# A router softmax on one core: VectorE and ScalarE run register loops over one softmax group a trip, and SyncE passes one word per load

## The chip, the cores and the metric

The kernel runs on one core of one Trainium2 chip. The time is the device time of one execution in microseconds (us); lower is better. The time of a kernel is the median over several executions. One further execution is recorded by the hardware profiler; its span (first to last recorded instruction) is a little shorter than its device time.

## The reference

```python
def setup_inputs():
    batch, seq, dim = 16, 512, 1024
    num_loras = 8
    return {
        "x": np.random.randn(batch, seq, dim).astype(np.float32),
        "router_weights": np.random.randn(dim, num_loras).astype(np.float32),
    }

def reference(x, router_weights):
    logits = np.matmul(x, router_weights)
    exp_logits = np.exp(logits - np.max(logits, axis=-1, keepdims=True))
    return (exp_logits / np.sum(exp_logits, axis=-1, keepdims=True)).astype(np.float32)
```

8192 tokens of 1024 values are multiplied with a 1024x8 matrix, and a softmax over the 8 results of each token follows. `x` is 33.55 MB, the output 0.26 MB.

## The kernel before

**Tiling.** Each of the 128 partitions holds 64 tokens. "Row j" below is the j-th token of all 128 partitions, a 128x1024 tile; there are 64 rows (J = 64). The list LOADS cuts rows 0 to 62 into transfers: 13 of four rows, three of two, five of one. Row 63 comes in three pieces of 512, 256 and 256 columns (PIECES).

**Loads.** The first four rows are loaded as fp32 by SyncE's DMA queue (L131) and cast to bf16 by ScalarE (`cast`, L333). All others are loaded by GpSimd's queue (L169, L182), which converts to bf16 on the way. GpSimd issues them one behind the other and has issued the last at about 17 us; from then on the DMA engines work the list down by themselves. Each of the 16 DMA engines adds 1 to a load's semaphore when its part has landed; 16 means landed.

**TensorE.** For a row it makes eight 128x128 transposes (a "turn", L276): five into the PSUM tile `ptv`, three into `pts`. VectorE copies `ptv` to SBUF (`dve_copy`, L376), ScalarE copies `pts` (`act_copy`, L350). Then TensorE makes eight small matmuls ("multiply", L263) whose result is 128x8 logits. There are two of each buffer. TensorE runs this as a loop of two rows a trip (L287 to L297) with the addresses in registers: two filler matmuls that keep the clock up, multiply of an odd row, a branch, turn of the next odd row, multiply of an even row, a wait for `s_in`, turn of the next even row, and the branch back (L297).

**Gates.** SyncE tells TensorE when a row has landed, row by row (L150 to L157). For an even row it adds 1 to `s_in`, for which TensorE waits ahead of the turn. For an odd row it waits until the buffer before was transposed (`s_tv`) and adds 1 to `s_c[1]`; TensorE's odd multiply waits for 3 there: the two copies of its own row and SyncE's word for the next odd row.

**Softmax.** After every eight rows (the first group has four) VectorE takes the maximum (L386), subtracts it (L390), ScalarE takes the exponential (L341), and VectorE sums, inverts and scales (L397, L401, L405), one of these steps behind each of the next rows' copies. VectorE and ScalarE have their whole program written out, one instruction per step and row. The tiles of a group come in pairs, used in turn.

**The end.** Rows 60 to 63 are handled alone (L303 to L328 on TensorE, L412 and L418 on VectorE, L343 on ScalarE). Row 63's pieces are transposed as they land (L310), copied out (VectorE L420, ScalarE L365), and multiplied (L324). Then come maximum, exponential, sum, inverse and scale of the last rows (L414, L345, L445, L447, L449), and the last 48 KB go out (L162). The first 208 KB go out at L160 when row 63's first piece has landed.

Of the kernel before, what the change touches and what calls it, by code (L numbers as in the profile page):

```python
# [11 lines left out]
def kernel(  # L12
# [6 lines left out]
    nc = tc.nc  # L19
    P = 128  # L20
    B, S, D = x.shape
    D2, N = router_weights.shape
    assert D2 == D
    M = B * S
    KO = D // P
    J = M // P
# [5 lines left out]
    fp32 = mybir.dt.float32  # L32
    bf16 = mybir.dt.bfloat16
    Exp = mybir.ActivationFunctionType.Exp
    X = mybir.AxisListType.X
    ALU = mybir.AluOpType
# [3 lines left out]
    LOADS = [4] * 13 + [2, 2, 2] + [1] * 5  # L40
    PIECES = [4, 2, 2]
    G, SKIP = 8, 4
    TRIPS = 31
    LOOP_T = 2 * TRIPS
    ALONE = 4
    NG = (J - ALONE + SKIP) // G
    starts = [max(0, G * g - SKIP) for g in range(NG)]
    ends = [G * (g + 1) - SKIP for g in range(NG)]
    DONE = ends[-2]
    assert sum(LOADS) == J - 1 and sum(PIECES) == KO and ends[-1] == J - ALONE  # L50
    VN, SN = 5, 3

    place = [16640]

    def sb(name, shape, dtype):
        size = mybir.dt.size(dtype)
        for n in shape[1:]:
            size *= n
        at = place[0]
        place[0] = -(-(at + size) // 64) * 64  # L60
        return nc.alloc_sbuf_tensor_at(name, shape, dtype, offset=at).ap()
# [8 lines left out]
    ident = sb("ident", [P, P], fp32)  # L70
    w8 = sb("w8", [KO, P, N], fp32)
    w_bf = sb("w_bf", [P, KO, N], bf16)
    outv = sb("outv", [P, J, N], fp32)
    filler = sb("filler", [P, 512], bf16)
    xTv = [sb(f"xTv{i}", [P, VN, P], bf16) for i in range(2)]
    xTs = [sb(f"xTs{i}", [P, SN, P], bf16) for i in range(2)]
    xTz = [sb(f"xTz{i}", [P, n, P], bf16) for i, n in enumerate(PIECES)]
    mx = [sb(f"mx{i}", [P, G, 1], fp32) for i in range(2)]
    ex = [sb(f"ex{i}", [P, G, N], fp32) for i in range(2)]
    ev = [sb(f"ev{i}", [P, G, N], fp32) for i in range(2)]  # L80
    ssum = [sb(f"ssum{i}", [P, G, 1], fp32) for i in range(2)]
    inv = [sb(f"inv{i}", [P, G, 1], fp32) for i in range(2)]
    low = sb("low", [P, ALONE], fp32)
    ev3 = sb("ev3", [P, ALONE, N], fp32)
    sum3 = sb("sum3", [P, ALONE, 1], fp32)
# [3 lines left out]
    LG_AT = 0x2000000  # L89
    lg = ps("lg", [P, 2, G, 64], fp32)  # L90
# [5 lines left out]
    sem = tc.alloc_semaphore  # L96
# [4 lines left out]
    s_ld = [sem(f"s_ld{i}") for i in range(len(LOADS))]  # L101
    s_z = [sem(f"s_z{i}") for i in range(len(PIECES))]
    s_cast = sem("s_cast")
    s_m = sem("s_m")
    s_d = sem("s_d")
# [5 lines left out]
    s_tv = sem("s_tv")  # L111
    s_ts = sem("s_ts")
    s_c = [sem(f"s_c{i}") for i in range(2)]
    s_in = sem("s_in")
    s_zt = [sem(f"s_zt{i}") for i in range(len(PIECES))]
    s_zc = [sem(f"s_zc{i}") for i in range(len(PIECES))]
    s_p = sem("s_p")
    s_ex = sem("s_ex")
    s_ev = sem("s_ev")
    s_low = sem("s_low")  # L120
    s_e3 = sem("s_e3")
    s_out = sem("s_out")
    s_st = [sem(f"s_st{i}") for i in range(2)]

# [21 lines left out]

    sp = nc.sync


    for j in range(2, J - 1):  # L150
        if j % 2:
            sp.wait_ge(s_tv, j - 1)
        if j < LOADS[0]:
            sp.wait_ge(s_cast, j + 1)
        elif j in first:
            sp.wait_ge(s_ld[first.index(j)], 16)
        sp.sem_inc(s_c[1] if j % 2 else s_in, 1)  # L157
    sp.wait_ge(s_z[0], 16)
    sp.wait_ge(s_out, NG - 1)
    sp.dma_start(out=out_rows[:, 0:DONE, :], in_=outv[:, 0:DONE, :]).then_inc(s_st[0], 16)  # L160
# [26 lines left out]
    pe = nc.tensor  # L187
# [22 lines left out]

    def loop_turn(b):

        for c in range(KO):
            t = again(
                turn_like,
                ins=(turn_like.ins[0], at([[J * D, P], [1, P]], xa, r_x[c])),
                outs=(pe.lower_ap(turn_ap(b, c), opt=False),),
            )
            if c == VN - 1:
                t.then_inc(s_tv, 1)  # L220
            if c == KO - 1:
                t.then_inc(s_ts, 1)
        pe.reg_add(r_l, r_l, 256)
        for c in range(KO):
            if c == KO // 2:
                pe.reg_alu(r_l, r_l, -4097, ALU.bitwise_and)
            pe.reg_add(r_x[c], r_x[c], D * 2)
# [7 lines left out]
                t.then_inc(s_ts, 1)  # L235
        return t

    def multiply(b, dst, want=2):

        for c in range(KO):  # L240
            if c == 0:
                pe.wait_ge(s_c[b], want).then_inc(s_c[b], -want)
            if dst is None:
                m = again(
                    mult_like,
                    ins=(
                        pe.lower_ap(w_bf[:, c, :], opt=False),
                        pe.lower_ap(chunk(b, c), opt=False, for_matmul_weights=True),
                    ),
                    outs=(at([[2 * G * 64, P], [1, N]], lg, r_l),),  # L250
                    start_tensor_calc=(c == 0),
                    stop_tensor_calc=(c == KO - 1),
                )
            else:
                m = pe.matmul(  # L255
                    dst, lhsT=chunk(b, c), rhs=w_bf[:, c, :],
                    start=(c == 0), stop=(c == KO - 1),
                )
            if c == KO - 1:
                m.then_inc(s_p, 1)  # L260
# [2 lines left out]
        return pe.matmul(spare, lhsT=filler[:, 0:P], rhs=filler, start=True, stop=True)  # L263


    w_ps = lg[:, 1, 0:N, 0:KO]
    pe.wait_ge(s_id, 1)
    pe.wait_ge(s_w, 16).then_inc(s_w, -16)  # L268
    for n in range(N):
# [2 lines left out]
    pe.wait_ge(s_fill, 1)  # L272
    mult_like = fill().ins
    pe.wait_ge(s_idb, 1)
    pe.wait_ge(s_cast, 2)
    turn_like = pe.transpose(turn_ap(0, 0), xa[:, 0, 0:P], identity).ins  # L276
    turn(0)
    pe.wait_ge(s_wb, 1)
# [8 lines left out]
    with nc.body("rows_multiply", valid_engines=only_pe):  # L287
        fill()
        fill()
        multiply(1, None, want=3)  # L290
        pe.br("rows_turn")
    with nc.body("rows_turn", valid_engines=only_pe):
        loop_turn(1)
        multiply(0, None)
        pe.wait_ge(s_in, 1).then_inc(s_in, -1)
        loop_turn(0)
        pe.br_lt(r_x[0], left_of(TRIPS - 1), on_true="rows_multiply", on_false="rows_done")  # L297
    nc.switch_bb("rows_done")
# [34 lines left out]
    def cast(i):  # L333
        act.wait_ge(s_f[i], 16).then_inc(s_f[i], -16)  # L334
        for k in (2 * i, 2 * i + 1):
            act.copy(xa[:, k, :], x_f32[:, k, :]).then_inc(s_cast, 1)  # L336

    def power(g):
        n = ends[g] - starts[g]
        act.wait_ge(s_ex, g + 1)  # L340
        act.activation(ev[g % 2][:, 0:n, :], ex[g % 2][:, 0:n, :], func=Exp).then_inc(s_ev, 1)  # L341

    def power_alone(k):  # L343
        act.wait_ge(s_low, k + 1)
# [1 line left out]
            ev3[:, k, :], alone[k], func=Exp, bias=low[:, k:k + 1]  # L346
        ).then_inc(s_e3, 1)

    def act_copy(j):
        act.wait_ge(s_ts, j + 1)  # L350
        act.copy(xTs[j % 2], pts[j % 2][:, 0:SN, :]).then_inc(s_c[j % 2], 1)  # L351

    cast(0)
    for j in range(J - 3):
        act_copy(j)
        if j == 1:
            cast(1)
        if j - 1 in ends[:-1]:
            power(ends.index(j - 1))
    power(NG - 1)  # L360
    act_copy(J - 3)
    power_alone(0)
    act_copy(J - 2)
    act.wait_ge(s_zt[0], 1)
    act.copy(xTz[0], z_bank[0]).then_inc(s_zc[0], 1)  # L365
    for k in range(1, ALONE):
# [6 lines left out]
    dve.wait_ge(s_wt, 1)  # L373
    dve.tensor_copy(out=w_bf, in_=w_ps.rearrange("p n ko -> p ko n")).then_inc(s_wb, 1)

    def dve_copy(j):  # L376
        dve.wait_ge(s_tv, j + 1)
        dve.tensor_copy(out=xTv[j % 2], in_=ptv[j % 2][:, 0:VN, :]).then_inc(s_c[j % 2], 1)  # L378

    def group(g):  # L380
        b, n = g % 2, ends[g] - starts[g]
        rows = lg[:, b, G - n:G, 0:N]

        def peak():
            dve.wait_ge(s_p, ends[g])
            dve.reduce_max(mx[b][:, 0:n, 0], rows, axis=X).then_inc(s_d, 1)  # L386

        def diff():
            dve.wait_ge(s_d, 3 * g + 1)
            dve.tensor_tensor(  # L390
                out=ex[b][:, 0:n, :], in0=rows, in1=mx[b][:, 0:n, :].broadcast_to([P, n, N]),
                op=ALU.subtract,
            ).then_inc(s_ex, 1)

        def total():
            dve.wait_ge(s_ev, g + 1)
            dve.reduce_sum(ssum[b][:, 0:n, 0], ev[b][:, 0:n, :], axis=X).then_inc(s_d, 1)  # L397

        def recip():
            dve.wait_ge(s_d, 3 * g + 2)  # L400
            dve.reciprocal(inv[b][:, 0:n, :], ssum[b][:, 0:n, :]).then_inc(s_d, 1)  # L401

        def scale():
            dve.wait_ge(s_d, 3 * g + 3)
            dve.tensor_tensor(  # L405
                out=outv[:, starts[g]:ends[g], :], in0=ev[b][:, 0:n, :],
                in1=inv[b][:, 0:n, :].broadcast_to([P, n, N]), op=ALU.mult,
            ).then_inc(s_out, 1)

        return [peak, diff, total, recip, scale]  # L410

    def low_alone(k):  # L412
        dve.wait_ge(s_p, J - ALONE + k + 1)
        dve.reduce_max(  # L414
            low[:, k:k + 1], alone[k], axis=X, negate=True
        ).then_inc(s_low, 1)
# [2 lines left out]
        dve.wait_ge(s_zt[i], 1)  # L419
        dve.tensor_copy(out=xTz[i], in_=z_bank[i]).then_inc(s_zc[i], 1)  # L420

    later = []
    for j in range(J - 3):
        dve_copy(j)
        if j in ends[:-1]:
            later += group(ends.index(j))
        if later:
            later.pop(0)()
    assert not later
    peak, diff, total, recip, scale = group(NG - 1)  # L430
    peak()
    diff()
    dve_copy(J - 3)
    total()
    low_alone(0)
    recip()
    dve_copy(J - 2)
    low_alone(1)
    dve_piece(1)
    dve_piece(2)  # L440
# [2 lines left out]
    scale()  # L443
    dve.wait_ge(s_e3, ALONE)
    dve.reduce_sum(sum3[:, :, 0], ev3, axis=X).then_inc(s_d, 1)  # L445
    dve.wait_ge(s_d, 3 * (NG) + 1)
    dve.reciprocal(inv3, sum3).then_inc(s_d, 1)  # L447
    dve.wait_ge(s_d, 3 * (NG) + 2)
    dve.tensor_tensor(  # L449
        out=outv[:, J - ALONE:J, :], in0=ev3, in1=inv3.broadcast_to([P, ALONE, N]), op=ALU.mult  # L450
    ).then_inc(s_out, 1)
# [30 lines left out]
```

## Time and profile before

| | |
|---|---|
| median of 5 executions | 86.80 us (86.69 to 86.83) |
| the profiled execution, device time | 86.81 us |
| its span | 85.5 us |
| busy share PE, PEld, DVE, ACT, POOL | 75%, 61%, 46%, 44%, 16% |
| read from HBM | 33.59 MB, 396 GB/s over the span |
| last landing of row 63's last piece | 81.73 us after the span's start |
| issue of the last output, its landing | 83.88 us, 85.44 us |

PE is TensorE's matmuls, PEld its weight loads, DVE VectorE, ACT ScalarE, POOL GpSimd, SP SyncE; a "q" behind an engine's name is its sequencer, the part that reads instructions and waits on semaphores. The profile cuts the span into 40 equal slices and gives the busy share of each in tenths. DMA traffic is listed by queue, and code that an engine fetches while it runs is a queue of its own, `q14 instruction`. The kernel converts on the way, so 1 byte written into SBUF stands for 2 read from HBM. All times in the text that stand alone ("at 80.55") are us from the span's start.

### The profile page before, as it was taken

The numbers are of one execution on the slowest core, as the hardware profiler recorded it, in microseconds if no ns is written. First come the engines' busy times: TensorE is split into PE (matmuls) and PEld (weight loads), VectorE is DVE, ScalarE is ACT, GpSimd is POOL, SyncE is SP. The second block draws the span as 40 slices with busy tenths as digits, with TensorE's granted clock in tenths as the row PEclk, the third lists the DMA queues.
The fourth block names the chain that finished last, engine by engine and source line by source line (L and its number), as shares of the span: only waits on it lengthen the run. The fifth ranks groups of instructions, "written<-read, shape, count | busy, mean of one in ns | idle before, by whom it ended". The sixth has DMA issues, their size and how long they took to land. (4 is left out here: it accounts for less than half of the span.)

```text
span 85.5 us, 2849 instructions
## 1 busy us (share of the span) xinstructions
PE 63.8 (75%) x1094; PEld 52.5 (61%) x1094; DVE 38.9 (46%) x114; ACT 38.0 (44%) x81; POOL 13.4 (16%) x30
## 2 busy tenths in 40 slices
PE   0052739999995977959289996959598699999860
PEld 0040727888774755838259884847476488777650
DVE  0020222566573543744225744636347257665662
ACT  0039384456453352534223644524427246545470
POOL 0489999800000000000000000000000000000000
PEclk9999999999999999999956999999999999999996
DMA  3999999999999999999999999999999999999920
GB/s 61 360 426 303 211 207 218 222 211 218 211 218 215 218 211 218 211 219 211 222 207 222 207 222 211 218 211 218 211 222 196 213 215 215 205 210 209 159 101 23
DMA packets 3906, 18.14 MB, mean 212 GB/s; under 512 B 568, under 2 KB 1080, under 8 KB 2112
## 3 DMA queue, kind: packets, MB, share of 16 engines
q0 software_dynamic: 3312, 15.73, 90.1%
q1 hardware_dynamic: 576, 2.36, 7.1%
q10 hardware_dynamic: 16, 0.03, 0.3%
q14 instruction: 2, 0.02, 0.0%
HBM read 33.59 MB, written 0.26 MB: 396 GB/s over the span
## 5 line engine op out<-in xcount | busy, mean ns | idle before, releaser
L351 ACT COPY xTs<-pts 128x384 bf16<-128x384 bf16 x63 | 30.1, 478 | 38.2 <-PE pts L276 36.8
L378 DVE COPY xTv<-ptv 128x640 bf16<-128x640 bf16 x63 | 31.0, 492 | 34.0 <-PE ptv L276 29.9
L276 PE MATMUL ptv<-identity,x_all 128*128 128x128 bf16 x311 | 29.1, 226 | 12.9 <-SPq L157 8.8
L276 PEld LDWEIGHTS ptv<-identity,x_all 128*128 (+1 forms) x311 | 19.2, 100 | 14.1 <-issue 14.0
L276 PE MATMUL pts<-identity,x_all 128*128 128x128 bf16 x186 | 21.5, 227 | 0.0
L263 PEld LDWEIGHTS lg<-w_bf,xTv 128*128 128x128 bf16 x305 | 15.7, 98 | 8.0 <-issue 1.5
L263 PE MATMUL spare<-filler 128*128 128x512 bf16 x61 | 19.5, 401 | 0.6
L263 PE MATMUL lg<-w_bf,xTv 128*128 128x8 bf16 x305 | 16.7, 168 | 0.0
L276 PEld LDWEIGHTS pts<-identity,x_all 128*128 x186 | 13.8, 102 | 0.0
L263 PE MATMUL lg<-w_bf,xTs 128*128 128x8 bf16 x183 | 13.2, 166 | 0.0
L169 POOL DMA_DIRECT2D x_all<-in_x_dram x20 | 10.7, 617 | 2.8 <-POOLq L144 2.8
L263 PEld LDWEIGHTS lg<-w_bf,xTs 128*128 128x128 bf16 x183 | 9.0, 96 | 0.0
L263 PEld LDWEIGHTS spare<-filler 128*128 128x128 bf16 x61 | 4.5, 101 | 2.3 <-issue 2.3
L270 PE MATMUL lg<-ident,w 8*128 8x8 f32 x8 | 1.0, 251 | 5.3 <-PEq L268 5.3
L270 PEld LDWEIGHTS lg<-ident,w 8*128 8x128 f32 x8 | 0.9, 197 | 5.3 <-issue 5.3
L336 ACT CAST x_all<-x_f 128x1024 bf16<-128x1024 f32 x4 | 4.0, 1044 | 0.0
L336 ACT ACT_TABLE_LOAD x1 | 1.3, 1283 | 5.6 <-ACTq L334 5.6
L386 DVE TENSOR_REDUCE mx<-lg 128x8 f32<-128x64 f32 (+1 forms) x8 | 1.8, 221 | 4.3 <-PE lg L263 4.3
L372 DVE CAST identity<-ident 128x128 bf16<-128x128 f32 x1 | 0.5, 518 | 5.3 <-POOL ident L175 5.3
L341 ACT ACTIVATE ev<-ex 128x64 f32<-128x64 f32 (+1 forms) x8 | 2.0, 253 | 1.1 <-DVE ex L390 1.0
L182 POOL DMA_DIRECT2D x_all<-in_x_dram x3 | 1.8, 707 | 0.0
L390 DVE TENSOR_TENSOR ex<-lg,mx 128x64 f32<-128x64 f32 (+1 forms) x8 | 1.7, 212 | 0.0
(41 smaller groups left out, 15.8 us busy)
## 6 DMA issues: line engine op xcount, KB each, us to landing
x_all<-in_x_dram POOLq DMA_DIRECT2D x12, 1024.0 KB, 32.6
x_f<-in_x_dram SPq DMA_DIRECT2D x2, 1024.0 KB, 6.3
x_all<-in_x_dram POOLq DMA_DIRECT2D x3, 512.0 KB, 60.3
x_all<-in_x_dram POOLq DMA_DIRECT2D x5, 256.0 KB, 64.4
out_dram<-outv SPq DMA_DIRECT2D x1, 208.0 KB, 1.9
x_all<-in_x_dram POOLq DMA_DIRECT2D x1, 128.0 KB, 66.0
x_all<-in_x_dram POOLq DMA_DIRECT2D x2, 64.0 KB, 65.8
out_dram<-outv SPq DMA_DIRECT2D x1, 48.0 KB, 1.6
```

The costliest lines, as they stand in the source:

```text
L169: nc.gpsimd.dma_start(out=xa[:, first[i]:first[i] + r, :], in_=x_rows[:, first[i]:first[i] + r, :]).then_inc(s_ld[i], 16)
L182: nc.gpsimd.dma_start(out=xa[:, J - 1, c], in_=x_rows[:, J - 1, c]).then_inc(s_z[i], 16)
L263: return pe.matmul(spare, lhsT=filler[:, 0:P], rhs=filler, start=True, stop=True)
L270: t = pe.transpose(w_ps[:, n, :], w8[:, :, n], ident[0:KO, 0:KO])
L276: turn_like = pe.transpose(turn_ap(0, 0), xa[:, 0, 0:P], identity).ins
L336: act.copy(xa[:, k, :], x_f32[:, k, :]).then_inc(s_cast, 1)
L341: act.activation(ev[g % 2][:, 0:n, :], ex[g % 2][:, 0:n, :], func=Exp).then_inc(s_ev, 1)
L351: act.copy(xTs[j % 2], pts[j % 2][:, 0:SN, :]).then_inc(s_c[j % 2], 1)
L372: dve.tensor_copy(out=identity, in_=ident).then_inc(s_idb, 1)
L378: dve.tensor_copy(out=xTv[j % 2], in_=ptv[j % 2][:, 0:VN, :]).then_inc(s_c[j % 2], 1)
L386: dve.reduce_max(mx[b][:, 0:n, 0], rows, axis=X).then_inc(s_d, 1)
L390: dve.tensor_tensor(out=ex[b][:, 0:n, :], in0=rows, in1=mx[b][:, 0:n, :].broadcast_to([P, n, N]), op=ALU.subtract,).then_inc(s_ex, 1)
```

## The change

VectorE's and ScalarE's written-out programs become loops of seven trips, one softmax group a trip, between four rows ahead and the last rows behind. In VectorE's loop two addresses are in registers: the half of the logits' tile (`r_b`, toggled each trip) and the place in the output (`r_o`). Semaphores that counted up over the whole program are now counted down by the waiter in each trip. The pairs of group tiles become single ones; the first group takes eight rows too, four of them empty places ahead of the output. Ahead of the loops VectorE makes 5 and ScalarE 11 increments of a semaphore `s_idle` for which nobody waits. SyncE adds the number of a load's rows to `s_in` once per load, and TensorE takes 1 off it ahead of every turn, odd ones too; the odd multiply waits only for its two copies. TensorE's first transposes wait for one cast row instead of two.

Counted instruction by instruction with branches, VectorE's program shrinks from 122 to 61, ScalarE's from 92 to 56, SyncE's from 76 to 39; TensorE's grows from 119 to 120, GpSimd's stays.

```diff
+    DVE_IDLE, ACT_IDLE = 5, 11
...
-    for j in range(2, J - 1):
-        if j % 2:
-            sp.wait_ge(s_tv, j - 1)
-        if j < LOADS[0]:
-            sp.wait_ge(s_cast, j + 1)
-        elif j in first:
-            sp.wait_ge(s_ld[first.index(j)], 16)
-        sp.sem_inc(s_c[1] if j % 2 else s_in, 1)
+    for j in range(LOADS[0]):
+        sp.wait_ge(s_cast, j + 1)
+        sp.sem_inc(s_in, 1)
+    for i, r in enumerate(LOADS):
+        if i:
+            sp.wait_ge(s_ld[i], 16)
+            sp.sem_inc(s_in, r)
...
     def loop_turn(b):
 
+        pe.wait_ge(s_in, 1).then_inc(s_in, -1)
         for c in range(KO):
...
-                pe.wait_ge(s_c[b], want).then_inc(s_c[b], -want)
+                pe.wait_ge(s_c[b], 2).then_inc(s_c[b], -2)
...
-        multiply(1, None, want=3)
+        multiply(1, None)
...
         multiply(0, None)
-        pe.wait_ge(s_in, 1).then_inc(s_in, -1)
         loop_turn(0)
...
+    for _ in range(ACT_IDLE):
+        act.sem_inc(s_idle, 1)
+    for i in range(2):
+        cast(i)
+        for j in (2 * i, 2 * i + 1):
+            act_copy(j, j)
+    act.wait_ge(s_ts, SKIP).then_inc(s_ts, -SKIP)
...
+    with nc.body("act_rows", valid_engines=only_act):
+        for k in range(G):
+            act_copy(k, k)
+            if k == 1:
+                act.wait_ge(s_ex, 1).then_inc(s_ex, -1)
+                power()
+        act.wait_ge(s_ts, G).then_inc(s_ts, -G)
+        act.reg_add(r_a, r_a, 1)
+        act.br_lt(r_a, NG - 1, on_true="act_rows", on_false="act_done")
...
+    dve.sem_inc(s_p, SKIP)
+    for _ in range(DVE_IDLE):
+        dve.sem_inc(s_idle, 1)
...
+    rows_at = dat([[2 * G * 64, P], [64, G], [1, N]], lg, r_b)
+    out_at = dat([[(SKIP + J) * N, P], [N, G], [1, N]], out_all, r_o)
...
+    with nc.body("dve_rows", valid_engines=only_dve):
+        for k in range(G):
+            dve_copy(k, k)
+            if k == 0:
+                dve.wait_ge(s_p, G).then_inc(s_p, -G)
+                peak()
+            elif k == 1:
+                diff()
+            elif k == 2:
+                dve.wait_ge(s_ev, 1).then_inc(s_ev, -1)
+                total()
+            elif k == 3:
+                recip()
+            elif k == 4:
+                scale()
+        dve.wait_ge(s_d, 3).then_inc(s_d, -3)
+        dve.wait_ge(s_tv, G).then_inc(s_tv, -G)
+        dve.reg_alu(r_b, r_b, 2048, ALU.bitwise_xor)
+        dve.reg_add(r_o, r_o, G * N * 4)
+        dve.br_lt(r_o, OUT_AT + (NG - 1) * G * N * 4, on_true="dve_rows", on_false="dve_done")
```

Behind the loops both engines go through the last rows in the order of before: VectorE copy of row 60, maximum, difference, copy of row 61, sum, and so on; ScalarE copy of row 60, exponential, copy of row 61, and so on.

## The prediction

> **What bounds the kernel now.** I read four views in this order: the slices, the queues, the chain that ended last with the waits of its stage, and the single DMA records. The slices and queues first:
>
> ```profile
> PEclk9999999999999999999956999999999999999996
> DMA  3999999999999999999999999999999999999920
> ...
> q0 software_dynamic: 3312, 15.73, 90.1%
> q1 hardware_dynamic: 576, 2.36, 7.1%
> q10 hardware_dynamic: 16, 0.03, 0.3%
> q14 instruction: 2, 0.02, 0.0%
> ```
>
> The DMA engines are full from slice 2 to slice 38 (about 81 us); no compute engine is. The loads set the pace: a four-row load lands every 4.87 us (17.74, 22.64, 27.49), while TensorE, when it has rows, does two in 1.73 us (fillers at 69.27, 71.00, 72.73). So it catches up and waits at each load; what matters is when the last loads land and what follows. The chain of work that ended last, in order of time, begins in a wait, just after row 62 has landed (80.41):
>
> ```profile
> 80.54 0.04 issue
> 80.58 0.44 PE ptv L276 x5
> 81.02 0.17 PE pts L276 x3
> 81.19 0.01 issue
> 81.20 0.38 PE pts L310 x4
> ```
>
> The timeline says the same: row 62's weight load comes 0.14 us after the landing, behind an idle gap.
>
> ```profile
> 80.55 0.29 PEld L276 LDWEIGHTS ptv<-identity,x_all 128*128 x5 [0.36 <-issue]
> ```
>
> Row 63's pieces land at 81.06, 81.39, 81.73 and are turned at 81.20, 81.62, 81.78. From there a chain of about 2.1 us to the last scale (ends 83.85), then the output (83.88 to 85.44). **Landings set the end.**
>
> Next, the landings one by one (16 increments per load, one per DMA engine): the last but one and the last.
>
> | load | last but one | last | apart |
> |---|---|---|---|
> | rows 24-27 | 37.19 | 37.20 | 0.01 |
> | rows 28-31 | 42.11 | 42.95 | 0.84 |
> | rows 32-35 | 46.94 | 47.32 | 0.38 |
> | rows 48-51 | 66.42 | 66.78 | 0.36 |
> | row 62 | 80.06 | 80.41 | 0.35 |
> | row 63, last piece | 81.42 | 81.73 | 0.31 |
>
> From rows 28-31 on one of the 16 engines is late, and stays late by 0.31 to 0.38. The DMA view, cut to 41 to 43 us, shows what else ran there:
>
> ```profile
> q0 software_dynamic: 68, 0.43, 103.2%
> q14 instruction: 1, 0.01, 1.0%
> ```
>
> A code fetch of 8192 bytes started at 41.58 and took 0.322 us. The second started at 49.93 and took as long; behind it no new last comes, but one of the faster engines moves from about 0.05 to about 0.2 behind the first. Each fetch costs its own DMA engine about its 0.32 us; the first fell on the engine that then ends the stream. The late rows 28-31 also explain the dip in PEclk:
>
> ```profile
> PE ptv L276 <- SPq L157: 8.8, 8, 1.9
> ```
>
> ```profile
> 41.00:46.00 5.00, 3.05 (x38) 2.43 (x35) 1.30 (x4) 0.96 (x2) 0.00 (x0) 0.71 1.03 216
> ```
>
> The first line is of the waits (total, times, longest): the longest, 1.9 us, is that one. The second is the window 41 to 46 us (busy time and count of each engine); its granted clock is 0.71. TensorE recovers long before the end.
>
> **Whose code?** SyncE stood still at 41.58 (its events are at 39.13 and 42.97), GpSimd was done, TensorE was in its loop. I counted the executed instructions, branches included. VectorE was held at its 54th from 40.87 until 43.85, and ScalarE at its 54th from 48.66 to 49.74. Both packets thus follow when an engine has come to its 54th, 0.7 and 1.3 us later. One count for both engines is what code blocks of 128 instructions (8192 bytes at 64) with equal preambles would give. The other reading is ScalarE at its 48th (since 41.03) and VectorE at its 63rd (since 48.91): two different counts, which I hold for less likely.
>
> **The change, part by part.**
>
> *Code.* New VectorE: the loop is instructions 25 to 44, the tail 45 to 61. New ScalarE: loop 35 to 47, tail 48 to 56. No loop contains a 54th. VectorE's 54th is now the copy of row 63's second piece, reached when the one before is dispatched (81.80 before the change); ScalarE's 54th is the second lone exponential, reached at 81.62. With the 0.7 and 1.3 us the packets run near 82.5, after the last landing (81.73) and beside the tail's compute. Nothing waits there for a load; neither fetch in the trace stalled its engine (ScalarE's copy at 50.39 shows the same idle 0.17 ahead of it as the one at 48.66). So both leave the stream, and the last landing is that of the next engine. Row 62 gains 80.41 - 80.06 = 0.35, the pieces 0.35, 0.35 and 0.31.
>
> Does TensorE keep up? Turn 61 begins at 79.47 today, behind the odd multiply that waited for row 61 (79.14). With row 61 at 78.82 and that multiply freed, it begins near 79.2, multiply 60 ends near 79.9, and row 62 (80.06 + 0.14 = 80.20) is waited for again. The chain behind shifts whole, by 0.31 to 0.35: **I take -0.33 us.**
>
> *Loop control.* A VectorE trip adds four semaphore instructions, two register operations and a branch, none of which the trace of before shows in a VectorE loop. Nearest rows: VectorE's semaphore instructions (21 ns), SyncE's back to back (0.06 apart), TensorE's register operations (32 to 69 ns, 0.1 apart), and
>
> ```profile
> L297 PEldq COMPARE_BRANCH  x31: 76/208/232, 13.0 to 81.0; - x31
> ```
>
> At the trip's end VectorE has 2 x 0.06 + 2 x 0.1 + 0.21 = 0.53 us, ScalarE 0.06 + 0.1 + 0.21 = 0.37, beside a copy still running (0.49 and 0.48). Trips end after rows 11, 19, ... 59, and the next row always opens a new load, so TensorE itself is waiting: VectorE idles over 1 us there in most trips. The tightest is the last: copy of row 59 at 77.79, next copy at 78.53; 77.79 + 0.53 = 78.32, 0.2 us to spare; ScalarE 77.96 + 0.37 = 78.33 against 78.70. Zero on the path, with bounds: below zero nothing, since no executed instruction goes; above, five times TensorE's branch (1.0 us) would move row 60's copy by 0.6, of which multiply 60 (79.89, the copy done at 79.02) absorbs all. Register addresses on three VectorE operations a trip: at most TensorE's 0.1 each, in idle time. Zero.
>
> *Idle increments.* ScalarE's 11 at 0.06 take 0.7 us between the barrier (2.8) and the first load's landing (5.5); VectorE's 5, one more and two register moves 0.6 between 6.6 and its first copy (9.87). Zero; without that cover they would delay row 0, which TensorE would make up at the next loads.
>
> *Gates.* The odd turn has a wait more. Behind it on TensorE stand the turn, multiply 0 and the even turn; its row is nearly always there. Its price is the row L295, 51 ns, in a trip that has 0.7 us to spare against the loads. SyncE no longer waits for `s_tv`, so its word can only be earlier. For row 62 the path load, SyncE, TensorE is as before: zero. Group tiles once instead of twice: the next group's first write comes eight rows behind the last reader; zero. Row 0 starts about 1 us sooner (one cast instead of two), not on the path.
>
> **A rule against the change.** TensorE's 31 backward branches in the trace go with no fetch packet at all, since the only two are accounted for. The Trainium skill, page "Runtime: NRT & Kernel Launch", section "Instruction fetch mechanics", says that code streams in sequentially with the fetch hidden, that a taken branch out of the two resident blocks forces a fetch, and that kernels therefore prefer unrolling; its blocks are 16 KiB. The trace's packets are 8 KiB, and "hidden" holds for the engine, not for the DMA engine that carries it. By the page's rule, if the loops missed, every back edge would stall.
>
> Sum: 86.81 (span 85.5 and 1.31 around it) - 0.33 = **86.48 us**. The profiled execution is within 0.01 of the median, so no correction.
>
> **Rivals.**
>
> 1. *The fetches are only moved, into the last loads.* Under the other count ScalarE's 48th is the first instruction behind its loop, reached at 77.96, fetch at about 78.5. The lag of its DMA engine was 0.84 in the load it hit and 0.35 one four-row load later. With 0.35 the end is as before: 86.8. With 0.84 still standing, 0.5 later: 87.3, slower. It decides if the fetch starts after about 76 and before 81.4. Against it: two counts are needed for one cause.
> 2. *The loops fetch at each back edge.* Six back edges on two engines are 12 packets of 0.32; six on the late DMA engine are 1.9 us against 0.33 saved: 88.4, and more if the engines stall. Against it: TensorE's loop.
> 3. *No difference.* The tail is held by something besides the late engine (another DMA engine slips, compute order): 86.65 to 86.95. The second fetch's engine had the slack to absorb it, so the lag may come back from other traffic.
> 4. *More than forecast.* The freed odd multiply and the earlier turn 61 pull the last group's steps ahead of the tail: at most turn 61's 0.27 less what is waited for again, some 0.1: 86.35.
>
> **Chances.** Forecast (86.40 to 86.60) 0.60; rival 4 0.06; rival 3 0.10; rival 1 0.16 (0.09 slower, 0.07 same); rival 2 and dearer loop control 0.08. Within 0.2% (0.17 us, about what a measurement of this kernel can tell from no change): faster 0.66, same 0.17, slower 0.17. The range 86.3 to 87.0 holds forecast, rivals 4 and 3 and half of rival 1.
>
> **What would show it.** Right: no `q14` packet of 8192 bytes between 0 and 81 us, one or two near 82.5; the last landing of a late load within 0.05 of the last but one; row 62's turn near 80.2; PEclk without the dip in slices 20 and 21; VectorE's gap ahead of row 60's copy still ended by TensorE. Wrong: a fetch packet between 76 and 81.4 (rival 1), one per trip (rival 2), or an even stream with an unmoved end (rival 3).

## The result, and the profile after

The changed kernel takes 86.56 us in the median (86.44 to 86.76, 29 executions) against 86.76 us (86.55 to 87.05, 49) for the kernel before in the same comparison: a ratio of 0.9979, 95% interval 0.9974 to 0.9984, or 0.2% faster. The forecast was 86.48 with a range of 86.3 to 87.0, so the time lies within the range, with 0.20 us of gain where 0.33 was forecast (from 86.81). The profiled execution takes 86.55 us with a span of 85.09 us, against 86.81 and 85.48. The span is shorter by 0.40, the time by only 0.26: some of the gain is given back outside the span, where 1.33 us became 1.46.

The page's slices and queues of the changed kernel:

```profile
PEclk9999999999999999999999999999999999999995
DMA  2899999999999999999999999999999999999920
...
q0 software_dynamic: 3312, 15.73, 90.5%
q1 hardware_dynamic: 576, 2.36, 7.1%
q10 hardware_dynamic: 16, 0.03, 0.1%
```

The line `q14 instruction` is gone: no code was fetched within the span. The dip in PEclk is gone as well. The DMA engines are as full as before. The DMA view from 41 to 43 us, where the first fetch stood, now shows the load queue alone:

```profile
DMA packets 69, 0.43 MB, mean 217 GB/s; under 512 B 16, under 2 KB 16, under 8 KB 16
...
q0 software_dynamic: 69, 0.43, 104.6%
```

The 16 landings of a load stay together: rows 28-31 land from 41.67 to 42.06 with the last two both at 42.06 (before: 42.11 and 42.95), row 62's last two at 80.02 and 80.03 (80.06 and 80.41), the last piece's at 81.37 and 81.38 (81.42 and 81.73). Row 62's turn and the start of the chain that ended last:

```profile
80.17 0.29 PEld L282 LDWEIGHTS ptv<-identity,x_all 128*128 x5 [0.48 <-issue]
```

```profile
80.15 0.04 issue
80.20 0.44 PE ptv L282 x5
80.64 0.17 PE pts L282 x3
80.80 0.02 issue
80.82 0.38 PE pts L315 x4
```

The turn still begins 0.14 us after the landing, behind an idle gap, and the whole chain has moved forward by 0.38 (80.58 to 80.20; the last scale 83.66 to 83.28; the output's issue 83.88 to 83.50). Landings set the end in both kernels.

### The profile page after: what moved, and what is told of

Its sections match the earlier page's. It is cut to its first block, busy times and chain, and to the rows that moved or that the text cites. A ratio compares the mean times of both kernels' runs of the same rounds, so it can differ in the third digit from the quotient of the medians.

```text
span 85.1 us, 2942 instructions
## 1 busy us (share of the span) xinstructions
PE 62.7 (74%) x1094; PEld 51.4 (60%) x1094; DVE 39.5 (46%) x114; ACT 37.9 (45%) x81; POOL 13.4 (16%) x30
## 5 line engine op out<-in xcount | busy, mean ns | idle before, releaser
L355 ACT COPY xTs<-pts 128x384 bf16<-128x384 bf16 x63 | 30.0, 476 | 37.4 <-PE pts L282 37.0
L282 PE MATMUL ptv<-identity,x_all 128*128 128x128 bf16 x311 | 28.3, 222 | 13.8 <-PEq L218 12.4
L282 PEld LDWEIGHTS ptv<-identity,x_all 128*128 (+1 forms) x311 | 18.5, 98 | 15.1 <-issue 15.1
L269 PE MATMUL spare<-filler 128*128 128x512 bf16 x61 | 19.0, 393 | 0.4
L423 DVE TENSOR_REDUCE mx<-lg 128x8 f32 x8 | 1.8, 225 | 4.4 <-DVEq L473 3.9
L344 ACT ACTIVATE ev<-ex 128x64 f32<-128x64 f32 x8 | 2.1, 257 | 1.6 <-DVE ex L423 0.9
L439 DVE TENSOR_REDUCE ssum<-ev 128x8 f32<-128x64 f32 x8 | 1.8, 220 | 0.1
```

Of the source, the lines that this page charges most:

```text
L344: return act.activation(ev, ex, func=Exp).then_inc(s_ev, 1)
L423: return dve.add_instruction(kind(name=f"I-{nc.next_id()}", engine=dve.engine, **k))
L439: dve.reduce_sum(ssum[:, :, 0], ev, axis=X).then_inc(s_d, 1)
```

## The experiments

Each kernel was run beside the kernel before on one chip. Spans are means over the runs compared, each on record to 0.1 us; "around" is the mean of time minus span. The three parts of the table are three chips, each with its own kernel before.

| kernel | median, us | ratio to before (95%) | span | around |
|---|---|---|---|---|
| before | 86.84 | | 85.53 | 1.32 |
| e1 gates only | 86.85 | 1.0006 (0.9997 to 1.0015) | 85.54 | 1.31 |
| e2 before, 58 idle on both | 86.83 | 1.0003 (0.9992 to 1.0013) | 85.55 | 1.31 |
| e3 changed, no idle (VectorE 56 long) | 86.63 | 0.9976 (0.9967 to 0.9985) | 85.25 | 1.35 |
| e4 VectorE's loop alone (61) | 86.95 | 1.0020 (1.0009 to 1.0031) | 85.51 | 1.45 |
| before | 86.77 | | 85.44 | 1.32 |
| e5 ScalarE's loop alone (VectorE 122) | 86.74 | 1.0000 (0.9991 to 1.0009) | 85.42 | 1.31 |
| e6 changed, VectorE idle 0 (56) | 86.48 | 0.9971 (0.9960 to 0.9982) | 85.19 | 1.31 |
| e7 changed, VectorE idle 12 (68) | 86.53 | 0.9972 (0.9963 to 0.9981) | 85.20 | 1.32 |
| e8 changed, 16 packets more (61) | 87.12 | 1.0047 (1.0034 to 1.0061) | 85.64 | 1.48 |
| before | 86.78 | | 85.47 | 1.31 |
| e9 changed, VectorE idle 8 (64) | 86.47 | 0.9963 (0.9950 to 0.9977) | 85.14 | 1.31 |
| e10 changed, VectorE idle 22 (78) | 86.48 | 0.9969 (0.9958 to 0.9980) | 85.16 | 1.34 |
| e11 the changed kernel again (61) | 86.65 | 0.9987 (0.9978 to 0.9996) | 85.20 | 1.46 |
| e12 changed, VectorE idle 0 (56) | 86.44 | 0.9961 (0.9947 to 0.9974) | 85.10 | 1.35 |

The theory was that the code fetches set the end; the rivals were that the gates did it, that a fetch costs nothing where it is hidden, and that the fetches are only moved.

### e1: the gates alone

```diff
+    for i, r in enumerate(LOADS):
+        if i:
+            sp.wait_ge(s_ld[i], 16)
+            sp.sem_inc(s_in, r)
...
-        multiply(1, None, want=3)
+        multiply(1, None)
```

on the kernel before, with TensorE's other waits as in the change; VectorE and ScalarE are unchanged.

> The kernel before with only the new gates of SyncE and TensorE; VectorE and ScalarE stay written out. Fetch theory (the end moves because the code fetches leave the load stream): two fetch packets of 8192 bytes remain near 41 and 50 us, rows 28-31 land 0.8 us late on one DMA engine, row 62's last landing stays near 80.4, span 85.4 to 85.5, time 86.7 to 86.8. Gate theory (the earlier words and the freed odd multiply make the gain): time 86.55 to 86.6 although the fetches remain.

Two fetches at 42.03 and 48.24; span 85.54 beside 85.53, ratio 1.0006. SyncE's own queue waits nearly always for a load now (66.9 us in total, against 37.4 before with 27.0 for TensorE), and that is worth nothing at the end. The gates are not the gain. The landings of the profiled execution do not look as expected: no single engine stands out by 0.3, and the landings of a load are wider apart from the start (0.53 us from first to last for rows 4-7, against 0.41 in the kernel before). Of the 16 landings of rows 28-31 five lie 0.25 or more behind the first, of rows 32-35 six, of rows 36-39 and of row 62 seven. The lags of the 16 behind the first add up to 3.22 in rows 16-19 and to 3.97 in rows 48-51, some 0.37 more for each fetch. So each fetch made one engine late, but neither of the two became the last: the spread was 0.54 in rows 24-27 and is 0.54 for row 62. The last piece lands at 81.59, and in e6's trace, which has no fetch and an equally wide start (0.57), at 81.55. What a fetch costs the end thus depends on how far ahead its engine was; in this execution it was next to nothing, and its span of 85.33 is the shortest of the eleven. So the picture of one late engine is that of one execution; the mean spans are the firmer reading, and they show the loss in full.

### e2: the fetches moved to the start, nothing looped

```diff
+    for _ in range(58):
+        act.sem_inc(s_idle, 1)
     cast(0)
...
     dve = nc.vector
+    for _ in range(58):
+        dve.sem_inc(s_idle, 1)
```

> The kernel before, with 58 idle semaphore increments ahead of VectorE's program and 58 ahead of ScalarE's, so that both programs are longer by 58 and nothing loops. Fetch theory with a fixed place in the program: both engines pass their place at about 5 to 6.5 us, the two packets come there, while the stream is not yet settled; the last landings are those of the changed kernel (row 62 near 80.05), span about 85.1, time 86.4 to 86.6 with loops nowhere. If the fetch goes by the length of the program or costs wherever it falls: last landings late by 0.3 as before, time 86.75 or more. Gate or loop theory: no change, 86.75.

The packets moved to 10.66 and 12.47 us. The DMA view of 10 to 13 us:

```profile
q0 software_dynamic: 92, 0.62, 101.2%
q14 instruction: 2, 0.02, 1.3%
```

So the fetch goes by the place in the program: 58 instructions more ahead of it moved it forward by 30 to 40 us. It does not follow at once: VectorE runs its 53rd instruction at 6.90 here and ScalarE at 5.91, so the packets come 3.8 us or more later. But the span is that of the kernel before, 85.55 beside 85.53. In the trace rows 4-7 have their last landing at 13.84 with the next at 13.19, and from rows 8-11 to the end one engine stays 0.16 to 0.18 behind. My expectation that an early fetch would be free was wrong: the stream is full from about 2 us on, and fetches at 10 to 13 us cost the mean span as much as those at 41 to 50.

### e3, e4, e5: whose fetch, and the idle increments

e3 is the changed kernel with both counts of idle increments at 0. e4 has ScalarE written out as before, VectorE in its loop; e5 has VectorE written out, ScalarE in its loop.

> The changed kernel without the idle increments (VectorE 56 instructions instead of 61, ScalarE 45 instead of 56). If the increments only place a fetch behind the program's end: same span (85.1), and time minus span moves from 1.45 us by 0.1 or more one way or the other. If they do nothing: 86.56 within 0.1 and no fetch packet. If they keep a loop inside a code block: fetch packets in each trip and a time over 87.

> The changed kernel with ScalarE written out again and only VectorE in a loop. Whose fetch is whose: if the packet at 41.6 is VectorE's and the one at 49.9 ScalarE's, one packet remains near 49 to 50 us, on an engine with slack, and the time is 86.55 to 86.6. If the one at 41.6 is ScalarE's, one packet remains near 41.6, rows 28-31 are late by 0.8 on one DMA engine, row 62 lands near 80.4, and the time is 86.75 or more. No packet at all: the place of a fetch does not go by the engine's own program.

> The changed kernel with VectorE written out again (122 instructions) and only ScalarE in a loop. Fetch theory: one fetch packet, VectorE's, at 41 to 43 us, and the landings behind it late on one DMA engine; span 85.4 to 85.5, time 86.75 to 86.85. If the whole gain came from ScalarE's loop and VectorE's fetch costs nothing: span 85.1 to 85.25, time 86.4 to 86.6. Time minus span 1.32 us, since VectorE is 122 long and not 61.

With VectorE's loop alone one packet remains, at 47.79; with ScalarE's alone one remains, at 41.46. e4's DMA view from 47 to 49 us:

```profile
q0 software_dynamic: 55, 0.45, 107.4%
q14 instruction: 1, 0.01, 1.0%
```

So the fetch at 41.58 in the kernel before was VectorE's and that at 49.93 ScalarE's. e5's DMA view from 41 to 43 us:

```profile
q0 software_dynamic: 66, 0.41, 99.3%
q14 instruction: 1, 0.01, 1.0%
```

The place can be read off more closely too: in e4 the packet ran at 47.79 while ScalarE had started its 52nd instruction and not its 53rd (47.92).

I had expected e4 to keep the gain, with the remaining packet on an engine with slack. It is 0.2% slower than the kernel before. Either fetch alone costs nearly the whole in the mean span: e4's span is 85.51 and e5's 85.42, beside 85.53 and 85.44 with both, and 85.25 and 85.19 (e3, e6) with none. This fits two DMA engines that are each made late by 0.3 to 0.4 us, where the later of them sets the end; both loops are needed. No run has both loops and one code fetch in the middle of the stream. That the fetches make the gain, and not the two loops as such, rests on the landings and on e8, which puts packets of that size back beside both loops. In e5's trace the lag shows as in the kernel before (rows 28-31: 42.06 and 42.83; last piece: 81.38 and 81.61). In e4's it is blurred: the last piece's late engine is 0.08 behind the next, while the slowest three are late by 0.14 to 0.22 against e3's, from a spread that was wider at rows 4-7 already (0.57 against 0.47). Against e6's trace, without a fetch and with the same 0.57, the last piece is late by 0.09 only (81.64 and 81.55). Why that spread differs between executions stays open.

e3 keeps the gain without increments. They therefore do not keep a loop inside a block.

### e6, e7, e9, e10: VectorE's length, and what happens behind the span

```diff
-    DVE_IDLE, ACT_IDLE = 5, 11
+    DVE_IDLE, ACT_IDLE = 0, 11
```

and 12, 8 and 22 for VectorE.

> The changed kernel without VectorE's 5 idle increments, ScalarE's 11 kept. The time around the span was 1.47 us in the changed kernel and with VectorE alone in a loop, 1.35 without any increments. If VectorE's length sets it: 1.32 to 1.35 here, span 85.1 to 85.25, time 86.45 to 86.6. If the increments of ScalarE set it: 1.47, time 86.55 to 86.7.

> The changed kernel with 12 idle increments on VectorE instead of 5 (68 instructions). If a longer VectorE program costs more behind the span: time minus span 1.47 or more. If only some lengths do: 1.32 to 1.35. A fetch packet within the span would put the length from which a third code block is fetched between 62 and 68; none is expected (92 has it, SyncE's 76 has not).

> The changed kernel with 8 idle increments on VectorE (64 instructions). With 5 (61) the time around the span is 1.47 us and no fetch packet is seen; with 12 (68) it is 1.32 and one packet runs at 80.85; with 0 (56) it is 1.32 and none runs. If the cost behind the span is a code block that VectorE asks for too late: a packet here between 81 and 84.5, and 1.32 to 1.47 around the span. If it goes by the length and not by the time: 1.47 and no packet.

> The changed kernel with 22 idle increments on VectorE: its loop is now instructions 42 to 61 and holds the place (about the 53rd) at which the fetches of the written-out programs were asked for. If a loop over that place sends for a block at each turn back (rival 2 of the prediction): 6 to 14 packets of 8192 bytes, VectorE waits at the loop's ends, time 87.5 to 90. If the block behind stays resident: one packet near 20 us, span as with one fetch, 85.4 to 85.5, time 86.7 to 86.8.

| VectorE's instructions | fetch packet at | around, us |
|---|---|---|
| 56 (e3, e6, e12) | none in the span | 1.31 to 1.35 |
| 61 (changed, e4, e8, e11) | none of VectorE's in the span | 1.45 to 1.48 |
| 64 (e9) | 84.86 | 1.31 |
| 68 (e7) | 80.85 | 1.32 |
| 78 (e10) | 80.92 | 1.34 |
| 122 (before, e1, e5) | 41 to 42 | 1.31 to 1.32 |

VectorE's length decides what lies around the span, and of the lengths run only 61 costs 0.15. The traces show no difference at the start: in the changed kernel, e3 and the kernel before the engines' first instructions start at the same times to 0.01 us, and each has six code packets of 8192 bytes ahead of the span. At 64 the fetch runs at 84.86, beside the last output, 0.3 us ahead of the span's end, later than the 81 to 84.5 I had expected, and 1.3 us after VectorE's last recorded instruction has ended (83.55). The DMA view of e9 from 84 to 85.2 us:

```profile
q1 hardware_dynamic: 144, 0.05, 15.4%
q14 instruction: 1, 0.01, 3.2%
```

This packet took 0.607 us and so ended 0.3 us behind the span, and the time around the span is 1.31 even so. At 61 it might come later still, wholly behind the span, where the end of the program could wait for it. That is an inference: no run shows the packet itself, and the cause of the 0.15 us stays open. At 56 none seems to be needed.

e7 and e10 answer two rivals. In e7, where I had expected no packet in the span, one runs while the last rows land, and the stream shows it only in the last piece (81.23, 81.36, 81.44 for its three last engines); the span is e6's to 0.01. In e10 the loop is instructions 42 to 61 and holds the 53rd, and still only one packet runs, at 80.92, after the loop has ended (I had expected several, or one near 20 us):

```profile
q14 instruction: 1, 0.01, 0.0%
```

So a loop across that place does not fetch at each turn, and the 53rd is not the whole rule. In e10 the place is passed in every trip without a packet, and in the changed kernel it is passed at about 81 us and none follows in the span. What makes the engine ask stays open; e7's and e10's packets came 3.05 us after the loop's last branch (77.79 and 77.87), but e9's came 6.99 us after it (77.87).

### e8: the disputed cost by itself

```diff
         if i:
             sp.wait_ge(s_ld[i], 16)
             sp.sem_inc(s_in, r)
+        if i == 7:
+            sp.dma_start(out=dummy[0:16, :, :], in_=x_rows[0:16, 0:2, :]).then_inc(s_dum, 16)
```

Besides these lines it has a spare tile, a semaphore and a wait for that semaphore at the very end.

> The changed kernel with 16 more packets of 8192 bytes, one for each of 16 partitions, read from x into a spare tile when rows 28-31 have landed (about 42 us); nothing reads them. If a packet of that size costs its DMA engine about its 0.3 us for good, and the landings set the end: span and time longer by 0.3 to 0.7 (these packets come by a data queue, 16 of them at once). If the stream has slack to make them up by its end: no change, time 86.5 to 86.65.

The 16 packets of 8192 bytes ran from 45.7 to 46.9 and took 0.322 us each (one 0.335), as the code fetches in the stream do. The window 45 to 47 us of e8, by queue:

```profile
q0 software_dynamic: 64, 0.39, 96.3%
q1 hardware_dynamic: 32, 0.13, 16.9%
```

Rows 32-35, under way then, land from 47.52 on instead of 46.54 (the changed kernel's trace); rows 36-39 are late by 0.35 (51.79 against 51.44), row 62 by 0.4 (80.44 against 80.03). The changed kernel itself was not run on this chip; the span is 0.45 longer than that of e6 and e7, which differ from it in VectorE's increments alone, and the time 0.6 longer, 0.15 of it around the span, as in the changed kernel. A packet of this size costs its DMA engine first about 1 us and then 0.35 to 0.4 us that the stream does not make up; with every engine hit, the end moves by all of it.

### e11 and e12: the best version beside the changed kernel

> The changed kernel once more, beside the next one on the same chip. If VectorE's 5 increments cost 0.15 us behind the span and nothing else: 0.1 to 0.15 us slower than without them (span equal, around it 1.47 against 1.32).

> The changed kernel without VectorE's increments, beside the one before on the same chip: 0.1 to 0.15 us faster than it, 0.3% faster than the kernel before. If the span grows by what is saved behind it: equal times.

On one chip the changed kernel takes 86.65 and the one without VectorE's increments 86.44: 0.21 less, of which 0.11 around the span and 0.10 in it. The share in the span I do not explain; spans of single runs differ by 0.2. Without the increments, or with 8, it beats both kernels: 0.9961 (0.9947 to 0.9974) and 0.9963 (0.9950 to 0.9977) against 0.9987 (0.9978 to 0.9996) in the same comparison.

## Why the prediction was right, and where not

**Landings set the end: shown.** The chain moved as a block with row 62's landing, 0.38 against 0.38 at that landing. In e8 a later stream moved the end by 0.45.

**The fetches leave the stream: right.** No packet runs in the span, and the mean span is shorter by 0.27 on e11's chip (0.24 to 0.37 over the loop kernels without a fetch ahead of 80 us), where I took 0.33.

**"Each fetch costs its own DMA engine about its 0.32 us": right in size** (0.35 to 0.4 in e8; by the sum of the lags, taken as in e1, 0.37 to 0.47 a fetch in the kernel before, e1, e4 and e5, while that sum changes by -0.18 to 0.05 in the eight traces with no fetch ahead of 80 us and no added packets). The second fetch's engine was misread: it moved not "to about 0.2 behind the first" but to about 0.4. In rows 32-35 seven of the 16 landings lie 0.2 or more behind the first, in rows 36-39 eight, and the one that is new stands at 0.40. So it lost about as much as the first. "[T]he first fell on the engine that then ends the stream", with the second absorbed by slack, does not hold beyond that one trace: in e4 the second alone kept the mean span where it was, and in e1's trace both were absorbed. By the prediction's own account VectorE's loop alone would have been enough; that the change looped both engines is what made the 0.33 come out.

**The 54th instruction: wrong in the count and as a rule.** The owners were right (e4, e5), but in e4 ScalarE's packet ran ahead of its 53rd, and a loop over that place (e10) does not fetch there. Taken from the time at which the engine came to its 53rd, the six packets of the kernel before, e1, e4 and e5 follow after 1.66 to 2.12 us; e2, e7, e9 and e10 do not fit even that. "[T]he packets run near 82.5, after the last landing" did not happen: none runs in the span. That the fetches left the stream was thus in part luck: the count by which it was forecast does not say when a packet runs.

**The term that was mis-sized is the one I carried over unchanged: "1.31 around it"** (1.33 with the profiled execution's unrounded span). It became 1.47 in the mean. I looked for the moved fetch only inside the span and took it as hidden beside the tail's compute. VectorE's 5 increments, costed at nothing, are what it depends on (e6, e12); what happens there stays open. So 0.33 less 0.15 would have been 0.18, and 0.20 was measured.

**Loop control: zero on the path, right, and priced too high.** I borrowed TensorE's branch, 208 ns. VectorE's own, of the changed kernel:

```profile
L488 DVEq COMPARE_BRANCH  x7: 50/56/56, 21.8 to 77.8; - x7
```

It takes 56 ns, ScalarE's 45; a register operation takes 45 and 35. The copy of row 60 comes 0.74 us behind that of row 59, as before.

**Gates: zero, shown by e1.** Turn 61 began at 78.96 instead of 79.47, more than the 0.27 forecast, and the end gained nothing from it, since row 62 is waited for again.

**The rivals.** Rival 1 (a fetch in the last loads) was priced at up to 0.5; in e7 a fetch at 80.85 cost at most 0.1 in the last landing. Rival 2 (a fetch at each back edge) fell with the changed kernel's own trace, which has no packet, and with e10, which has one. Rival 3 did not occur: the mean span is shorter in all seven runs of both loops without added packets. Rival 4 did not either: turn 61 came earlier and the end gained nothing from it.

**The dip in PEclk: likely right.** Of the 14 traces it stands in two, the two with the longest idle times of TensorE ahead of a turn in the settled stream (1.95 us in the kernel before, 2.1 in e8); e5, with 1.8, has none, nor have the others with 1.4 or less. e8's windows, with the granted clock in the third column from the end:

```profile
46.00:51.00 5.00, 2.91 (x44) 2.44 (x41) 1.52 (x5) 1.40 (x3) 0.00 (x0) 0.83 1.03 221
51.00:56.00 5.00, 5.00 (x83) 3.98 (x81) 2.86 (x8) 2.40 (x7) 0.00 (x0) 0.83 1.04 216
```

**The rule against the change** (the Trainium skill, "Runtime: NRT & Kernel Launch", section "Instruction fetch mechanics"). It holds fetches to be mostly hidden, and taken branches that leave the resident blocks to be costly. Here a fetch hides from the engine that asks (in the kernel before neither fetch stalled its engine) and not from a full DMA stream (e2, e4, e5), and 14 trips of two loops cost nothing on the path. No run shows a back edge that misses its block.

## What to carry to other kernels

When a stream of loads fills every DMA engine to the end, count each byte that the engines move besides it, the code of long written-out programs among them: one 8 KiB packet on one engine is about 0.4 us that this engine does not make up. Whether the end moves by it depends on how far ahead the engine was: by next to nothing in e1's trace, by 0.24 to 0.37 in the mean spans here. Look at the landings engine by engine, and at the spans of several executions, since one trace can put the loss on the wrong engine. And take the time around the span as a term of its own: here a few instructions more or fewer changed it by 0.15 us, for a reason that no run shows.

## What the runs showed that I had not expected

- A packet of 0.322 us that runs within about 1 us ahead of a load's landing delays that load on its DMA engine by 0.65 to 1.0 us (before: 42.95 against 42.11; e2: 13.84 against 13.19; e5: 42.83 against 42.06; e8: 47.52 against 46.54); of this 0.2 to 0.4 stays. Where it ran farther from a landing (before at 49.93, e4 at 47.79), no landing of the next load stands out so far.
- With VectorE's program of 61 instructions the time around the span is 0.10 to 0.17 us longer than with 56, 64, 68, 78 or 122.
- A compare-and-branch takes 56 ns on VectorE, 45 ns on ScalarE and 208 ns on TensorE (medians).
